# Prelude of a transformer block: the first modulation in blocks of 128 channels

## The chip, the cores and the metric

The kernel runs on one core of a Trainium2 chip, in one launch. The metric is device time in microseconds. Engines are named as in the profile: PE is TensorE (matmul), PEld its weight loads, DVE is VectorE, ACT is ScalarE, POOL is GpSimd, and SP is the queue that issues most transfers.

## The reference

One transformer block over 1024 tokens of width 1024, batch 1, fp32. What the prelude computes:

```python
mod = silu(c) @ w_mod + b_mod                       # c: [1, 1024], w_mod: [1024, 6 * 1024]
shift1, scale1, gate1, shift2, scale2, gate2 = split(mod, 6)
xn = x * rsqrt(mean(x * x, -1) + 1e-6) * ln1_g
u = xn * (1 + scale1) + shift1                      # [1024 tokens, 1024 channels]
proj = u @ w_in                                     # 5384 columns
```

`proj` feeds an attention branch, a linear-recurrence branch and gates; after them come an output projection, a second normalisation and a feed-forward part. Two column groups of `w_in` of 128 columns each, 24 and 25 in the kernel's numbering, are the low-rank projections of the recurrence; they are needed first.

## The kernel before

Channels lie on the 128 partitions and tokens along the free dimension, so u is held as `u_hi` and `u_lo` of shape [128, 8, 1024]: eight blocks of 128 channels (`kt`), two halves of 512 tokens (`half`). Each fp32 matrix is split into a rounded part (hi) and a remainder (lo), and a product is three products: hi hi, hi lo, lo hi.

The prelude is the `with` block that opens the pools `st` and `stp` (L403 to L545). In it the orders of SP, DVE and ACT are those of the program text, and PE's is so in the whole kernel. Instructions that follow in the text but lie outside the block may still be placed between them on SP, DVE, ACT and POOL, where the program's scheduler sees room.

- `load_x` (L408) loads eight tiles of 128 tokens, 512 KB each. `square` (L415) sums squares on ACT, `norm_x` (L421) makes 1/rms on ACT (`rms_rstd`, L285) and diagonal matrices `dg` on DVE (L426).
- `turn` (L456) multiplies x by `dg` on PE, which transposes and normalises: four fp32 products fill one PSUM bank for one block and one half. ACT copies it to `uf` (L511).
- `mod_load` (L428) loads eight tiles of w_mod for one part of the modulation, each 128 rows by 1024 columns. `mod_add` (L440) accumulates them on DVE: `acc = w[kt] * sc[kt] + acc` over 1024 columns, with `sc` = silu(c). `mod_sum` (L446) adds the partitions with eight one-column products on PE (`mps`) and adds the bias; for the scale it also forms `A1` = (1 + scale) * ln1_g. The scale (i = 1) is summed first, then the shift (i = 0).
- `u_steps` (L462): DVE applies A1 and the shift in place (L468), ACT rounds to `u_hi` (L469), DVE takes the remainder `u_lo` (L472).
- `low_part` (L475) multiplies u with both low-rank weights into four PSUM banks (`low`). Their own split is L527 (ACT) and L534 (DVE).
- `low_out` (L488) mixes neighbouring tokens of the result into `xwa` and `xg`.
- `warm(n)` (L435) issues n products into a bank that nobody reads.

The text of the prelude runs stage by stage: all squares and turns; the scale over all channels; the shift over all channels; then u and the low-rank products for half 0 and half 1. SP's order is x, the scale's tiles, the shift's tiles, the two low-rank weights, `w2`, `g2` and further constants.

After it comes the first large product, `ps_rkv`, by `shifted` (L346) with weights from `load_w` (L245): a load into one of two `raw` buffers (L249), a cast on ACT (L261), a remainder on DVE (L263). Those `raw` buffers are shared with the low-rank weights and `w2`. POOL makes `w2l` (L540) from `w2` and its cast (L537).

Of the kernel before, what the change touches and what calls it, by code (L numbers as in the profile page):

```python
# [44 lines left out]
NC1 = 384  # L45
# [86 lines left out]
def hybrid_block(ctx: ExitStack, tc: tile.TileContext, a, out):  # L132
    nc = tc.nc
# [3 lines left out]
    def mm(o, lhsT, rhs, start, stop, more=False):  # L137

        weave.mm_cost(o, lhsT, rhs)
        nc.tensor.matmul(o, lhsT, rhs, start=start, stop=stop, skip_group_check=more)  # L140
# [12 lines left out]
    rp = ctx.enter_context(tc.tile_pool(name="rp", bufs=2))  # L153
# [3 lines left out]
    wp = ww_st.enter_context(tc.tile_pool(name="wp", bufs=2, side="right"))  # L157
# [3 lines left out]
    cst = cp.tile([128, NC1], F32R, name="cst")  # L161
# [3 lines left out]
    def V(name, i=0, n=1):  # L165
        o, _ = VEC[name]
        return vec[:, o + i : o + i + n]
# [6 lines left out]
    ident, ones = f32(eye_r), f32(C("ones"))  # L174
# [16 lines left out]
    sc = cp.tile([128, 8], F32, name="sc")  # L191
# [112 lines left out]
    A1 = cp.tile([128, 8], F32, name="A1")  # L304
    m1 = cp.tile([128, 16], F32, name="m1")
# [3 lines left out]
    u_hi = upool.tile([128, KT, S], F32R, name="u_hi")  # L309
    u_lo = upool.tile([128, KT, S], F32R, name="u_lo")  # L310
# [24 lines left out]
    with ExitStack() as es:  # L335
# [67 lines left out]
        with tc.tile_pool(name="st", bufs=1) as st, tc.tile_pool(name="stp", bufs=2, space=PS) as stp, \  # L403
# [11 lines left out]
            def square(half, xs, js):  # L415
                for j in js:
                    t = half * 4 + j
                    nc.scalar.activation(uf[1][:, 6:8, :].rearrange("p k s -> p (k s)"), xs[j], AF.Square,
                                         accum_out=ssq[:, t : t + 1])

            def norm_x(half):  # L421

                hs = slice(half * 4, half * 4 + 4)
                rms_rstd(rstd[:, hs], ssq[:, hs])
                for j in range(half * 4, half * 4 + 4):
                    ts(dg[:, j, :], ident, rstd[:, j : j + 1], None, op0=ALU.mult)  # L426

            def mod_load(i, tags):  # L428
                ws = [st.tile([128, D], F32, tag=tags[kt % len(tags)], name=f"wm{i}{kt}", bufs={"mw": 4, "xt": 8}[tags[kt % len(tags)]])
                      for kt in range(KT)]  # L430
                for kt, w in enumerate(ws):
                    nc.sync.dma_start(w, a["w_mod"][kt * 128 : kt * 128 + 128, i * D : i * D + D])
                return ws, st.tile([128, D], F32, name=f"acc{i}")

            def warm(n):  # L435

                for _ in range(n):
                    mm(idle[:, 0:NC1], cst[:, 0:128], cst, start=True, stop=True)

            def mod_add(kt, ws, acc):  # L440
                if kt == 0:
                    ts(acc, ws[kt], sc[:, 0:1], None, op0=ALU.mult)
                else:
                    stt(acc, ws[kt], sc[:, kt : kt + 1], acc, op0=ALU.mult, op1=ALU.add)

            def mod_sum(i, acc):  # L446
                for j0 in (0, 4):
                    ps = stp.tile([128, 4], F32, tag="mp", name=f"mps{i}{j0}")
                    for j in range(4):
                        c0 = (j0 + j) * 128  # L450
                        mm(ps[:, j : j + 1], acc[:, c0 : c0 + 128], ones[:, 0:1], start=True, stop=True)
                    tt(m1[:, i * 8 + j0 : i * 8 + j0 + 4], ps, V("b_mod", i * 8 + j0, 4), op=ALU.add)
                    if i == 1:
                        stt(A1[:, j0 : j0 + 4], m1[:, 8 + j0 : 12 + j0], 1.0, V("ln1_g", j0, 4), op0=ALU.add, op1=ALU.mult)

            def turn(kt, half, xs):  # L456
                ps = stp.tile([128, NH], F32, tag="tp", name=f"tr{half}_{kt}")
                for j in range(4):
                    mm(ps[:, j * 128 : j * 128 + 128], xs[j][:, kt * 128 : kt * 128 + 128], dg[:, half * 4 + j, :], start=True, stop=True)
                return ps  # L460

            def u_steps(half):  # L462

                cs = slice(half * NH, half * NH + NH)
                for kt in range(KT + 1):
                    if kt < KT:
                        x = uf[half][:, kt, :]
                        ts(x, x, A1[:, kt : kt + 1], m1[:, kt : kt + 1], op0=ALU.mult, op1=ALU.add)  # L468
                        nc.scalar.copy(u_hi[:, kt, cs], x)  # L469
                    if kt > 0:  # L470
                        k = kt - 1
                        tt(u_lo[:, k, cs], uf[half][:, k, :], f32(u_hi[:, k, cs]), op=ALU.subtract)  # L472
                        yield k

            def low_part(kt, half, parts):  # L475
                for (wh, wl), ps in zip(low, low_ps):
                    for i in parts:
                        w, x = ((wh, u_hi), (wh, u_lo), (wl, u_hi))[i]
                        mm(ps[half], w[:, kt * 128 : kt * 128 + 128], x[:, kt, half * NH : half * NH + NH],
                           start=kt == 0 and i == 0, stop=kt == KT - 1 and i == 2)  # L480
# [21 lines left out]
            xs = [load_x(half) for half in range(2)]  # L502
            m = [mod_load(1, ("mw",)), None]
            uf = [st.tile([128, KT, NH], F32, name=f"uf{half}") for half in range(2)]
            warm(28)
            for half in range(2):
                square(half, xs[half], range(4))
                norm_x(half)
            for half in range(2):
                for kt in range(KT):  # L510
                    nc.scalar.copy(uf[half][:, kt, :], turn(kt, half, xs[half]))  # L511
            m[1] = mod_load(0, ("xt", "mw"))
            low_raw = [low_w(24, wp, ("whi", "wlo"), 2), low_w(25, st, ("xt", "xt"), 8)]
            low = [x[1:] for x in low_raw]
            w2 = rp.tile([128, S], F32, tag="raw", name="w2")
            for r in range(2):
                for j in range(2):
                    nc.sync.dma_start(w2[r * 64 : r * 64 + 64, j * 512 : j * 512 + 512], a["w2a2"][j * 64 : j * 64 + 64, :])
            nc.sync.dma_start(g2, a["g2"])
            nc.sync.dma_start(cst2, a["cst"][:, NC1:])  # L520
            for i in (1, 0):
                for kt in range(KT):
                    mod_add(kt, *m[1 - i])
                mod_sum(i, m[1 - i][1])
                warm((6, 40)[i])
            for raw, hi, _ in low_raw:
                nc.scalar.copy(hi, raw)  # L527
            low_ps = [[stp.tile([128, NH], F32, tag=("low", "tp")[hf], name=f"low{j}{hf}") for hf in range(2)] for j in range(2)]
            for half in range(2):
                for kt in u_steps(half):  # L530
                    low_part(kt, half, (0, 1))
                    if half == 0 and kt in (3, 5):
                        raw, hi, lo = low_raw[kt == 5]
                        tt(lo, raw, f32(hi), op=ALU.subtract)  # L534
                for kt in range(KT):
                    low_part(kt, half, (2,))
            nc.scalar.copy(w2h, w2)  # L537
# [1417 lines left out]
```

## Time and profile before

| What | us |
|---|---|
| Median of 3 runs (1702.5 to 1705.13) | 1702.53 |
| The profiled run's own time | 1703.54 |
| Its span, first to last instruction | 1701.4 |
| Transfers in the first 40 us | 13.81 MB |

A row of a timeline or of the chain begins with its start in us from the span's start and its duration; a group's row gives count, total busy time and the mean duration of one in ns. An instruction's duration is longer than the distance to the next independent one, since they overlap. In a row of windows the numbers are the stretch, its length, the busy time of PE, PEld, DVE, ACT and POOL with counts, the clock granted to TensorE, the share of the 16 transfer engines that was busy, and GB/s. A chain is what ended last, followed back; idle time of an engine counts only if it lies on it.

### The profile page before, as it was taken

The numbers are of one execution on the slowest core, as the hardware profiler recorded it, in microseconds if no ns is written. First come the engines' busy times: TensorE is split into PE (matmuls) and PEld (weight loads), VectorE is DVE, ScalarE is ACT, GpSimd is POOL, SyncE is SP. The second block draws the span as 40 slices with busy tenths as digits, with TensorE's granted clock in tenths as the row PEclk, the third lists the DMA queues.
The fourth block names the chain that finished last, engine by engine and source line by source line (L and its number), as shares of the span: only waits on it lengthen the run. The fifth ranks groups of instructions, "written<-read, shape, count | busy, mean of one in ns | idle before, by whom it ended". The sixth has DMA issues, their size and how long they took to land.

```text
span 1701.4 us, 26280 instructions
## 1 busy us (share of the span) xinstructions
PE 1649.4 (97%) x9886; PEld 1351.3 (79%) x9886; DVE 1216.2 (71%) x2390; ACT 810.2 (48%) x1482; POOL 145.7 (9%) x175
## 2 busy tenths in 40 slices
PE   7999999998999999999999999999999999999998
PEld 6767777686877777988878888888888888888886
DVE  5776786778676633888877634897777777787677
ACT  5553334434444555766642323654444444454455
POOL 0010101110111003123112000000000000000000
PEclk9999999999999999999999999999999999999999
DMA  8487743533332226443277611133332233484453
GB/s 328 146 307 210 189 121 97 134 109 107 91 115 76 83 89 151 139 120 100 75 272 269 238 62 63 50 106 98 120 111 100 93 118 101 152 296 150 128 211 114
DMA packets 120975, 239.87 MB, mean 141 GB/s; under 512 B 39888, under 2 KB 48336, under 8 KB 120848
## 3 DMA queue, kind: packets, MB, share of 16 engines
q1 hardware_dynamic: 112896, 220.94, 39.4%
q0 software_dynamic: 7952, 17.25, 3.7%
q8 instruction: 78, 1.28, 0.3%
q14 instruction: 49, 0.40, 0.1%
HBM read 172.59 MB, written 65.54 MB: 140 GB/s over the span
## 4 chain that ended last, share of the span: by engine, by line
PE 78%; DVE 10%; DMA 5%; ACT 3%; SPq 2%; issue 1%; DVEq 0%; ACTq 0%
PE X L140 13%; PE D L140 12%; PE Y L140 6%; PE wo L140 5%; PE br L140 5%; PE gt L140 5%; PE ps_rkv L140 4%; PE rk_ps L140 4%; PE W L140 3%; PE lg L140 2%; PE v L140 2%; PE ov L140 2%; PE qk L140 2%; PE sp L140 2%; PE tp L144 2%; PE tr L140 2%
## 5 line engine op out<-in xcount | busy, mean ns | idle before, releaser
L140 PE MATMUL D<-op,op 128*128 128x512 f32 x924 | 209.8, 389 | 0.0
L140 PEld LDWEIGHTS D<-op,op 128*128 128x128 f32 x924 | 173.3, 188 | 36.3 <-DVE op L1218 0.3
L140 PE MATMUL X<-T_m,S 128*128 128x512 f32 x440 | 107.2, 390 | 0.1
L140 PEld LDWEIGHTS X<-T_m,S 128*128 128x128 f32 x440 | 82.4, 188 | 18.2 <-ACT T_m L1643 0.6
L1217 ACT CAST op<-g 128x512 fp32r<-128x512 f32 x77 | 47.8, 621 | 73.4 <-PE D L140 48.2
L1218 DVE TENSOR_TENSOR op<-g,op 128x512 fp32r<-128x512 f32 x77 | 53.0, 688 | 41.3 <-ACT op L1217 41.3
L769 DVE TENSOR_TENSOR t<-E,M 128x60 f32<-128x60 f32 (+24 forms) x248 | 57.3, 231 | 33.1 <-DMA M<-sm 27.8
L1454 DVE SCALAR_TENSOR_TENSOR c<-ab,vec,c 128x512 f32<-128x512 f32 x88 | 65.9, 749 | 19.5 <-ACT c L1457 18.0
L263 DVE TENSOR_TENSOR lo_in<-raw_in,hi_in 128x512 fp32r<-128x512 f32 x84 | 56.4, 706 | 32.0 <-PE gt L140 13.8
L1418 DVE TENSOR_TENSOR S<-ur,S 128x512 fp32r<-128x512 f32 x66 | 45.5, 691 | 35.6 <-ACT S L1414 35.4
L1414 ACT CAST S<-ur 128x512 fp32r<-128x512 f32 x66 | 41.0, 622 | 55.5 <-DVE ur L1407 30.6
L261 ACT CAST hi_in<-raw_in 128x1024 fp32r<-128x1024 f32 x42 | 43.9, 1049 | 47.9 <-PE ps_rkv L140 16.8
L1418 DVE TENSOR_TENSOR A<-ur,A 128x512 fp32r<-128x512 f32 x64 | 44.0, 688 | 30.9 <-ACT A L1414 30.7
L140 PE MATMUL Y<-T_h,A 128*128 128x512 f32 x264 | 63.5, 389 | 0.0
L140 PE MATMUL Y<-T_h,S 128*128 128x512 f32 x264 | 63.3, 389 | 0.0
L140 PE MATMUL X<-B_b,A 128*128 128x512 f32 x252 | 60.8, 390 | 0.0
L140 PE MATMUL W<-B_f,A 128*128 128x512 f32 x252 | 60.6, 389 | 0.0
L771 DVE TENSOR_TENSOR E<-E,t 128x60 f32<-128x60 f32 (+24 forms) x248 | 53.8, 217 | 5.8
L1039 ACT ACTIVATE P<-lg,nm 128x896 f32<-128x896 f32 (+3 forms) x64 | 47.5, 744 | 21.9 <-DVE nm L1035 21.7
L140 PEld LDWEIGHTS Y<-T_h,A 128*128 128x128 f32 x264 | 49.6, 188 | 10.4
L140 PEld LDWEIGHTS Y<-T_h,S 128*128 128x128 f32 x264 | 49.6, 188 | 10.3
L1414 ACT CAST A<-ur 128x512 fp32r<-128x512 f32 x64 | 39.9, 623 | 34.3 <-PE X L140 31.5
(469 smaller groups left out, 4179.6 us busy)
## 6 DMA issues: line engine op xcount, KB each, us to landing
raw_in<-in_w_in SPq DMA_DIRECT2D x50, 512.0 KB, 4.1
wm<-in_w_mod SPq DMA_DIRECT2D x48, 512.0 KB, 6.6
ur<-in_w_up SPq DMA_DIRECT2D x44, 512.0 KB, 4.2
g<-d_g SPq DMA_DIRECT2D x35, 512.0 KB, 3.7
d_g<-gs SPq DMA_DIRECT2D x44, 256.0 KB, 2.0
d_g<-c SPq DMA_DIRECT2D x33, 256.0 KB, 4.6
d_st<-qh SPq DMA_DIRECT2D x64, 128.0 KB, 2.5
d_gate<-gs SPq DMA_DIRECT2D x32, 256.0 KB, 2.8
```

Of the source, the lines that this page charges most:

```text
L140: nc.tensor.matmul(o, lhsT, rhs, start=start, stop=stop, skip_group_check=more)
L144: nc.tensor.transpose(o, i, eye)
L261: nc.scalar.copy(hi, raw)
L263: nc.vector.tensor_tensor(lo[:, c : c + NH], raw[:, c : c + NH], f32(hi[:, c : c + NH]), op=ALU.subtract)
L769: tt(tv, E32[:, 0:J, s : s + 1].to_broadcast([128, J, W]), M32[:, s : s + 1, s + 1 : 32].to_broadcast([128, J, W]), op=ALU.mult)
L771: tt(E32[:, 0:J, s + 1 : 32], E32[:, 0:J, s + 1 : 32], tv, op=ALU.add)
L1039: nc.scalar.activation(e[:, 0:n], lg[:, 0:n], AF.Exp, bias=nm[:, 0:1], accum_out=nm[:, 1:2])
L1217: nc.scalar.copy(hi, src)
L1218: tt(lo, src, f32(hi), op=ALU.subtract)
L1414: nc.scalar.copy(hi, src)
L1418: tt(lo, src, f32(hi), op=ALU.subtract)
L1454: stt(c, ab[:, x + hf * NH : x + hf * NH + NH], V("conv_w", 22 * x + i), c, op0=ALU.mult, op1=ALU.add)
```

## The change

The modulation is cut by output channels. For block `kt`, `mod_load(kt)` loads two tiles of 512 KB, shift and scale, each holding all 1024 inputs for 128 output channels; a row of such a tile in memory is a run of 512 B. The scale is now summed by eight products per block on PE that accumulate in one PSUM column (`mod_scale`). The shift stays on DVE, in eight steps of 128 columns (`mod_shift`), with one product to add the partitions (`mod_sum`). `mod_col` forms the block's column of the shift and of A1. `u_upper` applies both on ACT, straight from the turn's PSUM bank, and rounds; `u_lower` takes the remainder on DVE. The low-rank products follow block by block, with all three parts at once. The low-rank weights' loads and splits come ahead of the second half of x, the splits around the first turn; w_mod has nine buffers, and the loads of blocks 4 to 7 are issued in the loop. `w2`, `g2` and the constants are loaded in block 4, and `w2` is cast in block 6. `warm` is called with 34, 10 and 16 in place of 28, 6 and 40.

```diff
-            def mod_add(kt, ws, acc):
-                if kt == 0:
-                    ts(acc, ws[kt], sc[:, 0:1], None, op0=ALU.mult)
-                else:
-                    stt(acc, ws[kt], sc[:, kt : kt + 1], acc, op0=ALU.mult, op1=ALU.add)
...
+            def mod_load(kt):
+
+                ws = [st.tile([128, D], F32, tag="mw", name=f"wm{i}{kt}", bufs=9) for i in range(2)]
+                for i, w in enumerate(ws):
+                    nc.sync.dma_start(w.rearrange("p (c n) -> p c n", n=128),
+                                      a["w_mod"].rearrange("(c p) n -> p c n", p=128)[:, :, i * D + kt * 128 : i * D + kt * 128 + 128])
+                return ws
...
+            def mod_scale(kt, ps):
+                for ci in range(KT):
+                    mm(ps[:, 1:2], mw[kt][1][:, ci * 128 : ci * 128 + 128], sc[:, ci : ci + 1], start=ci == 0, stop=ci == KT - 1)
+
+            def mod_shift(kt):
+                acc = st.tile([128, 128], F32, tag="acc", name=f"acc{kt}", bufs=2)
+                for ci in range(KT):
+                    w = mw[kt][0][:, ci * 128 : ci * 128 + 128]
+                    if ci == 0:
+                        ts(acc, w, sc[:, 0:1], None, op0=ALU.mult)
+                    else:
+                        stt(acc, w, sc[:, ci : ci + 1], acc, op0=ALU.mult, op1=ALU.add)
+                return acc
+
+            def mod_sum(kt, ps, acc):
+                mm(ps[:, 0:1], acc, ones[:, 0:1], start=True, stop=True)
+
+            def mod_col(kt, ps):
+                tt(m1.rearrange("p (i k) -> p k i", i=2)[:, kt, :], ps[:, 0:2],
+                   V("b_mod", 0, 16).rearrange("p (i k) -> p k i", i=2)[:, kt, :], op=ALU.add)
+                stt(A1[:, kt : kt + 1], m1[:, 8 + kt : 9 + kt], 1.0, V("ln1_g", kt), op0=ALU.add, op1=ALU.mult)
...
+            def u_upper(kt, half, ps):
+
+                uf[kt, half] = st.tile([128, NH], F32, tag="uf", name=f"uf{half}_{kt}", bufs=3)
+                nc.scalar.activation(uf[kt, half], ps, AF.Identity, scale=A1[:, kt : kt + 1], bias=m1[:, kt : kt + 1])
+                nc.scalar.copy(u_hi[:, kt, half * NH : half * NH + NH], uf[kt, half])
+
+            def u_lower(kt, half):
                 cs = slice(half * NH, half * NH + NH)
...
+                tt(u_lo[:, kt, cs], uf[kt, half], f32(u_hi[:, kt, cs]), op=ALU.subtract)
+
+            def low_part(kt, half):
+                for i in (0, 2, 1):
+                    for (wh, wl), ps in zip(low, low_ps):
                         w, x = ((wh, u_hi), (wh, u_lo), (wl, u_hi))[i]
...
+            def low_split(n, engine):
+                raw, hi, lo = low_raw[n]
+                if engine == "ACT":
+                    nc.scalar.copy(hi, raw)
+                else:
+                    tt(lo, raw, f32(hi), op=ALU.subtract)
+
+            def mods(kt):
+                ps = pb.tile([128, NH], F32, tag="big", name=f"mod{kt}")
+                mod_scale(kt, ps)
+                acc = mod_shift(kt)
+                mod_sum(kt, ps, acc)
+                mod_col(kt, ps)
...
+            uf = {}
+            xs = load_x(0)
+            mw = [mod_load(0)]
+            low_raw = [low_w(24, wp, ("whi", "wlo"), 2), low_w(25, st, ("hi25", "lo25"), 1)]
...
+            xs += load_x(1)
+            mw += [mod_load(kt) for kt in range(1, 4)]
+            warm(34)
+            for t in range(4):
+                square(t)
+            norm_x(0)
+            low_ps = [[stp.tile([128, NH], F32, tag="low", name=f"low{j}{hf}", bufs=4) for hf in range(2)] for j in range(2)]
+            mods(0)
+            low_split(0, "ACT")
+            u_upper(0, 0, turn(0, 0))
+            warm(10)
+            low_split(0, "DVE")
+            low_split(1, "ACT")
+            low_split(1, "DVE")
+            blocks = [(kt, half) for kt in range(KT) for half in range(2)]
+            for n, (kt, half) in enumerate(blocks):
+                if n == 0:
+
+                    u_lower(kt, half)
+                    low_part(kt, half)
+                    for t in range(4, 8):
+                        square(t)
+                    norm_x(1)
+                    warm(16)
+                if n < len(blocks) - 1:
+                    u_upper(*blocks[n + 1], turn(*blocks[n + 1]))
+                if n:
+                    u_lower(kt, half)
+                    low_part(kt, half)
+                if half == 0 and kt < KT - 1:
+                    mods(kt + 1)
+                    if kt < 4:
+                        mw.append(mod_load(kt + 4))
+                if kt == 4 and half == 0:
...
+                if n == 12:
+                    nc.scalar.copy(w2h, w2)
```

More of the change, by code (lines that the diff above doesn't have):

```diff
@@ L413, in load_x, with square @@
                 return xs
[L415 to L419, printed above, removed]
+            def square(t):
+                nc.scalar.activation(u_lo[:, 6 + t // 4, :], xs[t], AF.Square, accum_out=ssq[:, t : t + 1])
             def norm_x(half):
@@ L438, in warm @@
                     mm(idle[:, 0:NC1], cst[:, 0:128], cst, start=True, stop=True)
-            def mod_add(kt, ws, acc):
-                if kt == 0:
-                    ts(acc, ws[kt], sc[:, 0:1], None, op0=ALU.mult)
-                else:
[L444 to L454, printed above, removed]
@@ L457, in turn @@
+            def mod_sum(kt, ps, acc):
[4 more added lines that the diff above has]
+                stt(A1[:, kt : kt + 1], m1[:, 8 + kt : 9 + kt], 1.0, V("ln1_g", kt), op0=ALU.add, op1=ALU.mult)
+            def turn(kt, half):
                 ps = stp.tile([128, NH], F32, tag="tp", name=f"tr{half}_{kt}")
@@ L458, in turn @@
                 for j in range(4):
-                    mm(ps[:, j * 128 : j * 128 + 128], xs[j][:, kt * 128 : kt * 128 + 128], dg[:, half * 4 + j, :], start=True, stop=True)
+                    mm(ps[:, j * 128 : j * 128 + 128], xs[half * 4 + j][:, kt * 128 : kt * 128 + 128], dg[:, half * 4 + j, :], start=True, stop=True)
                 return ps
-            def u_steps(half):
-                cs = slice(half * NH, half * NH + NH)
[L465 to L473, printed above, removed]
@@ L500, in hybrid_block @@
             dg = xwa.rearrange("p (j s) -> p j s", s=128)
             idle = pb.tile([128, NH], F32, tag="big", name="idle")
[L502 to L511, printed above, removed]
@@ L521, in hybrid_block @@
[L521 to L536, printed above, removed]
@@ new lines, in hybrid_block @@
+            mods(0)
[24 more added lines that the diff above has]
+                if kt == 4 and half == 0:
+                    w2 = rp.tile([128, S], F32, tag="raw", name="w2")
+                    for r in range(2):
+                        for j in range(2):
+                            nc.sync.dma_start(w2[r * 64 : r * 64 + 64, j * 512 : j * 512 + 512], a["w2a2"][j * 64 : j * 64 + 64, :])
+                    nc.sync.dma_start(g2, a["g2"])
+                    nc.sync.dma_start(cst2, a["cst"][:, NC1:])
+                if n == 12:
+                    nc.scalar.copy(w2h, w2)
```

21 lines of the change are left out of this document (1 added, 20 removed).

## The prediction

> **What bounds the kernel now.** I read the page first, then the chain of waits over the first 120 us, then the timeline of that stretch by engine, then groups and windows for prices.
>
> ```profile
> span 1701.4 us, 26280 instructions
> PE 1649.4 (97%) x9886; PEld 1351.3 (79%) x9886; DVE 1216.2 (71%) x2390; ACT 810.2 (48%) x1482; POOL 145.7 (9%) x175
> ```
>
> TensorE is busy for 97% of the span, so a microsecond taken from the prelude only counts if the moment from which TensorE runs without gaps comes earlier. That moment is the first product of `ps_rkv`; its row, and the last low-rank row before it, from the timeline:
>
> ```profile
> 71.33 3.84 PE L140 MATMUL low<-u_hi,lo_in 128*128 128x512 f32 x16
> ...
> 75.01 1.99 PE L140 MATMUL ps_rkv<-u_hi,hi_in 128*128 128x512 f32 x8
> ```
>
> So the prelude ends at 75.0 us. What made it that long, from the chain:
>
> ```profile
> 9.97 0.07 ACT uf L418
> ...
> 12.76 1.16 ACT uf L418 x2
> 13.94 1.16 ACT uf L418 x2
> ...
> 16.30 0.31 ACT rstd L287
> ...
> 16.84 0.48 ACT uf L511
> ...
> 17.36 13.05 PE tr L140 x112
> ...
> 33.41 1.30 DVE acc L444
> ...
> 41.34 1.30 DVE acc L444
> ...
> 62.32 1.06 ACT hi_in L261
> ```
>
> The stages stand one behind the other: TensorE turns x until 30.4, VectorE sums the shift from 32.6 to 42.6 with TensorE on filler, then VectorE makes u and the low-rank products trail it. The last row is a cast of the next stage's weights on ScalarE: it lies in that queue between two casts of u, and ScalarE had stood waiting for its transfer.
>
> **The change: TensorE.** A product of two fp32 operands shows as two records: `mod_sum` issues 8 products, and its row has 16.
>
> ```profile
> 30.37 1.95 PE L140 MATMUL mps<-cst,acc 128*128 128x1 f32 x16
> ```
>
> One such product costs 1.95 / 8 = 0.244 us though it has a single column. A `turn` (4 products, 8 of the 112 records in 13.05 us) costs 0.93. A low-rank product costs (75.01 - 71.33) / 16 = 0.230. The change adds 64 products for the scale (15.6 us) and keeps 8 sums in place of 16 (-1.95); turns and low-rank products stay in number. It also drops filler: 60 instead of 74 matmuls. For one block of channels TensorE now has 2 turns (1.86), 12 low-rank products (2.76), 8 scale products (1.95) and one sum (0.24): **6.82 us**, and its order is fixed, so the next block cannot overtake.
>
> **The change: VectorE and ScalarE.** VectorE loses the scale's eight passes and the 16 in-place affine steps (L468), and gets the shift in 64 small steps.
>
> ```profile
> L444 DVE SCALAR_TENSOR_TENSOR acc<-wm,sc,acc 128x1024 f32<-128x1024 f32 x14 | 18.0, 1285 | 3.2 <-DMA wm<-in_w_mod 2.7
> L1454 DVE SCALAR_TENSOR_TENSOR c<-ab,vec,c 128x512 f32<-128x512 f32 x88 | 65.9, 749 | 19.5 <-ACT c L1457 18.0
> L771 DVE TENSOR_TENSOR E<-E,t 128x76 f32<-128x76 f32 x8 | 1.9, 236 | 0.2
> 11.72 0.87 DVE L426 TENSOR_SCALAR xwa<-cst,rstd 128x128 f32<-128x128 f32 x4 [8.45 <-ACT rstd L288]
> L426 DVE TENSOR_SCALAR xwa<-cst,rstd 128x128 f32<-128x128 f32 x8 | 1.7, 282 | 12.7 <-ACT rstd L288 12.7
> L472 DVE TENSOR_TENSOR u_lo<-uf,u_hi 128x512 fp32r<-128x512 f32 x16 | 11.0, 686 | 0.6 <-ACT u_hi L469 0.5
> L469 ACT CAST u_hi<-uf 128x512 fp32r<-128x512 f32 x16 | 9.6, 619 | 12.1 <-DVE uf L468 12.1
> L1329 ACT ACTIVATE uf_e<-tr,m,A 128x512 f32<-128x512 f32 x8 | 6.2, 787 | 8.3 <-PE tr L140 8.3
> L527 ACT CAST hi_in<-raw_in 128x1024 fp32r<-128x1024 f32 x2 | 2.1, 1044 | 10.3 <-DMA raw_in<-in_w_in 10.3
> ```
>
> No row has a 128x128 step of this form. The line through 1024 and 512 elements gives 0.35 us at 128; the 76-element row bounds it below at 0.24. In a dependent chain 0.04 is added (six steps of L444 from 33.41 to 41.34 are 1.32 apart, each 1.285). Eight steps, the first 0.28 + 0.04: 2.2 to 3.0 us; I take 3.0, the line of the same operation. The affine step moves to ScalarE, straight from PSUM, at 0.79 (L1329 is the same operation) in place of a 0.59 copy. Per block VectorE has 3.0 + 2 x 0.6 + 0.4, ScalarE 2 x (0.79 + 0.62): both lie beside TensorE's 6.82. The wait to check is the round trip. From the start of a turn: 0.93, affine 0.79, cast 0.62, u_lo 0.69, shift 3.0, handoffs 0.2 make 6.2, and TensorE reaches that sum at 6.58. It holds with 0.35 us to spare; shift steps over 0.40 us would end that.
>
> **The change: transfers.** The bytes are the same, but each w_mod tile now comes as 1024 pieces of 512 B in place of 128 of 4 KB. The nearest row is the d_v store, whose pieces are 512 B; beside it two stretches of w_mod reads in 4 KB rows:
>
> ```profile
> DMA packets 1056, 0.52 MB, mean 87 GB/s; under 512 B 32, under 2 KB 1056, under 8 KB 1056
> 357.50:358.00 0.50, 0.50 (x14) 0.43 (x16) 0.50 (x2) 0.00 (x0) 0.00 (x0) 1.00 0.97 293
> 18.00:29.00 11.00, 11.00 (x98) 11.00 (x97) 8.12 (x7) 6.83 (x12) 0.00 (x0) 1.00 0.90 294
> 29.00:40.00 11.00, 10.36 (x69) 9.90 (x67) 9.03 (x11) 1.38 (x3) 0.00 (x0) 1.00 1.01 404
> ```
>
> With the engines full, 512 B pieces moved at 293 GB/s and 4 KB rows at 404. I take 293 for reads too; the bounds are 404, and half of 293 for a read that no row shows. A pair of tiles (1.05 MB) then takes 3.6 us (a tile 1.8), under 6.82, so transfers bind only at the start. The Trainium skill ("DMA: Bandwidth & Descriptors", Specifications) puts the least size for full rate at 512 B; by that a pair would take 2.6 us, the sum below would stay (VectorE's first shift, not the transfer, ends last there), and the second rival would lose its chance to the forecast. The row, a store, speaks for less than full rate.
>
> On SP the two low-rank weights pass four x tiles, which come 1.05 MB / 404 = 2.6 us later; the square steps they feed wait for ScalarE until 19.5 anyway. The loads of blocks 4 to 7 wait on SP for buffers that shift and scale of earlier blocks free; behind them stand w2, g2, the second constants and the first weights of `ps_rkv`, all needed only from about 63 us (the cast of w2 in block 6). POOL keeps its two w2l steps.
>
> **The sum.** The fourth x tile is there at 9.97 (its square starts). Block 0's tiles follow at 13.55. VectorE ends dg at 12.6 and shift 0 at 15.6; TensorE ends scale 0 at 15.5, its sum at 15.95 and the first turn at 16.9. ScalarE then has affine 0.79, cast 0.62, the second weight's cast 1.04, four squares 1.18 apart and 0.54 for the rstd: 24.7. dg lets the second turn run from 25.0 to 25.95, scale 1 until 27.9, but shift 1 (25.6 to 28.6) ends last; its sum ends at 28.95. Six blocks of 6.82 follow: 69.85. Behind the sum of block 7 stand turn, low-rank, turn, low-rank (4.62: 74.5); the last half's u_lo is ready at 73.1 + 0.79 + 0.62 + 0.69 + 0.15 = 75.35, and two products more make 75.8. That is 0.8 later than 75.01. The weights cast that sat in ScalarE's and VectorE's queues (1.06, then 1.29) will sit somewhere in the new loop too, against 0.35 to spare: +0.9. The low-rank outputs now all come at the end: 0 to 0.75, taken as 0.3. Together **+2.0 us**: a span of 1703.4, 1705.5 for the profiled run (1703.54 with its span of 1701.4), 1704.5 against the median of 1702.53.
>
> What 15.6 us of scale products add on TensorE thus eats nearly all that the overlap of the stages wins.
>
> **Rivals.** First, *a cast of weights stalls the loop* (slower). The raw buffer of the first `ps_rkv` weights is free once the low-rank weights are split, about 20.6, so the load can be issued there, behind the last x tile (13.55 + 2.6 + 5.2 = 21.4) and nine w_mod tiles: 21.4 + 9 x 1.8 + 1.3 for itself = 39 until it lands. If its cast sits early in ScalarE's queue, everything behind it stands. Before, this wait was:
>
> ```profile
> ACT hi_in L261 <- DMA raw_in<-in_w_in: 3.5, 1, 3.5
> 42.77 2.99 PE L140 MATMUL mps<-cst,acc 128*128 128x1 f32 x16 [3.41 <-DVE acc L444]
> 44.00:45.00 1.00, 1.00 (x7) 1.00 (x6) 0.16 (x1) 0.00 (x0) 0.00 (x0) 0.50 0.00 0
> 49.00:50.00 1.00, 1.00 (x4) 0.81 (x3) 1.00 (x3) 0.62 (x1) 0.00 (x0) 0.50 0.00 0
> ```
>
> A wait as long again costs 3.5 less 0.8: 1707. A cast placed at 27.5 waits 11 us, and after the gap of 3.41 us the granted clock was 0.50 until 50, some 7 us, 3.5 us more: 1718. Middle: 1711. It decides from a wait of some 2.5 us. For it: it happened before; against: with more in its queue the load may be placed later.
>
> Second, *512 B reads at half the store's rate*, 146 GB/s: a pair takes 7.2 us, all w_mod (8.39 MB) takes 57.5 us, and behind the first x tiles (9.97) and beside 3.15 MB at 404 (7.8) block 7 lands at 75.3; with 1.95, 0.24 and the 6.0 from there to the end the prelude ends at 83.5: 1711. For it: no row shows such a read. Against it: the slower stretch of 4 KB reads still made 294 on engines 0.90 full.
>
> Third, *the summing products are cheap* (faster): were one product in an accumulating group 0.12 (its neighbour's load hidden) and a shift step 0.27, a block would take 5.7, the prelude end near 68.5: 1697. Against it: in the row of `mps` 8 products left 16 records 0.122 apart, and each has its own weights.
>
> **Numbers.** Forecast 0.48, stalled cast 0.27, slow reads 0.14, cheap products 0.11. About 0.2% (3.4 us) is what a measurement tells from no change: 1699.1 to 1705.9. The forecast's own spread (-3 to +3) leaves 0.42 within and 0.06 above; the two slower rivals give 0.39 above and 0.02 within; the third 0.11 below. Range 1699 to 1713; the forecast's own is 1701.5 to 1707.5.
>
> **What would show it.** Right: 128 records of 128x1 for the scale (two per product), 0.12 apart; starts of the last sums of two blocks 6.8 us apart; TensorE without gaps from about 29; first `ps_rkv` product at 75 to 77. The cast: an idle time of ScalarE before L261 that ends with raw_in. Reads: TensorE's scale products waiting for wm. Wrong altogether: a period clearly under 6.8 us, or a first `ps_rkv` product before 72.

## The result and the profile after

| | before | after |
|---|---|---|
| median (runs; lowest to highest) | 1702.25 us (6; 1700.97 to 1705.13) | 1715.26 us (6; 1713.60 to 1719.88) |
| ratio, 95% interval | | 1.0067 [1.0054, 1.008] |
| profiled run, its span | 1703.54, 1701.4 | 1715.42, 1713.2 |
| mean granted clock of that run | 0.990 | 0.986 |
| first `ps_rkv` product | 75.01 | 88.04 |

One of the nine runs of a_pin_wide below took 4140.17 us; medians and ratios leave it out.

The change made the kernel 13 us slower, 10.8 us above the forecast and 2.3 above the range. All of it is there when the prelude ends. These rows of TensorE's timeline of the changed kernel (start, duration, engine, operation; idle time before it and what ended it) are the summing products of blocks 1, 2, 4, 5, 6 and 7, the first product after the longest idle time, and the first product of the next stage:

```profile
29.06 0.38 PE L140 MATMUL mod<-cst,acc 128*128 128x1 f32 x2 [0.65 <-DVE acc L450]
...
37.26 0.36 PE L140 MATMUL mod<-cst,acc 128*128 128x1 f32 x2
...
50.45 0.36 PE L140 MATMUL mod<-cst,acc 128*128 128x1 f32 x2
...
58.24 1.22 PE L140 MATMUL low<-u_hi,hi_in 128*128 128x512 f32 x2 [4.14 <-ACT u_hi L471]
...
64.23 0.56 PE L140 MATMUL mod<-cst,acc 128*128 128x1 f32 x2
...
73.72 0.36 PE L140 MATMUL mod<-cst,acc 128*128 128x1 f32 x2
...
81.34 0.38 PE L140 MATMUL mod<-cst,acc 128*128 128x1 f32 x2 [0.88 <-DVE acc L450]
...
88.04 1.99 PE L140 MATMUL ps_rkv<-u_hi,hi_in 128*128 128x512 f32 x8
```

The sum of block 1 came at 29.06, where the forecast had 28.95. From block 2 to block 4 two periods took 50.45 - 37.26 = 13.19, 6.60 each (forecast 6.82). Then one block took 13.78 and the next 9.49. The idle time of 4.14 us ends with a cast of `u` on ScalarE. ScalarE's timeline shows what held that cast up, and the chain of waits what it waited for:

```profile
48.35 0.62 ACT L471 CAST u_hi<-uf 128x512 fp32r<-128x512 f32 x1
55.81 1.04 ACT L261 CAST hi_in<-raw_in 128x1024 fp32r<-128x1024 f32 x1 [6.84 <-DMA raw_in<-in_w_in]
56.76 0.77 ACT L470 ACTIVATE uf<-tr,m,A 128x512 f32<-128x512 f32 x1
```

```profile
49.23 6.56 DMA raw_in<-in_w_in
```

The cast of the next stage's first weights stands in ScalarE's queue behind the rounding of `u` of block 3, second half, which ended at 48.97. Its load was issued only at 49.23, so ScalarE stood for 6.84 us, and behind the cast stood the affine step of block 4. SP's queue says why the load came so late: it lies behind the last w_mod tile, four pieces of w2, g2 and the second constants (start, duration on the queue).

```profile
44.48 3.54 SPq L560 DMA_DIRECT2D w<-in_w2a  x4
48.06 0.58 SPq L561 DMA_DIRECT2D g<-in_g  x1
48.69 0.43 SPq L562 DMA_DIRECT2D cst<-in_cst  x1
```

The gap cost more than itself. In the windows of the changed kernel (stretch; its length; busy time and instructions of PE, PEld, DVE, ACT, POOL; granted clock; DMA share; GB/s) the clock is at half from 57 to about 70:

```profile
57.00:60.00 3.00, 1.76 (x4) 1.49 (x5) 2.86 (x7) 2.45 (x4) 0.00 (x0) 0.50 0.23 55
60.00:63.00 3.00, 3.00 (x14) 2.72 (x13) 1.68 (x5) 0.00 (x0) 0.00 (x0) 0.50 0.32 120
63.00:66.00 3.00, 3.00 (x15) 3.00 (x16) 0.92 (x3) 0.00 (x0) 0.00 (x0) 0.50 0.00 0
66.00:69.00 3.00, 3.00 (x10) 2.50 (x9) 0.79 (x2) 1.40 (x2) 0.00 (x0) 0.50 0.01 3
69.00:72.00 3.00, 3.00 (x15) 2.67 (x14) 2.56 (x8) 1.15 (x2) 0.00 (x0) 0.76 0.02 5
```

There are two shorter drops earlier, at 16 to 19 and at 29 to 33, with no idle time of more than 0.65 us beside them:

```profile
16.00:18.00 2.00, 2.00 (x10) 2.00 (x10) 1.32 (x3) 0.35 (x1) 0.00 (x0) 0.50 1.03 410
18.00:20.00 2.00, 2.00 (x10) 2.00 (x9) 0.00 (x0) 1.97 (x4) 0.00 (x0) 0.69 1.01 394
...
30.00:32.00 2.00, 2.00 (x9) 1.81 (x9) 0.44 (x1) 0.74 (x1) 0.00 (x0) 0.50 1.19 294
```

So there were two suspects: the cast that waits (rival 1 of the prediction), and a clock that falls for some other reason. The experiments separate them.

### The profile page after: what moved, and what is told of

It reads as the page before. It is cut to its first block, busy times and chain, and to the rows that moved or that the text cites. A ratio compares the mean times of both kernels' runs of the same rounds, so it can differ in the third digit from the quotient of the medians.

```text
span 1713.2 us, 26506 instructions
## 1 busy us (share of the span) xinstructions
PE 1665.3 (97%) x9984; PEld 1367.0 (80%) x9984; DVE 1213.0 (71%) x2432; ACT 813.1 (47%) x1482; POOL 143.5 (8%) x175
## 4 chain that ended last, share of the span: by engine, by line
PE 80%; DVE 9%; DMA 4%; ACT 3%; SPq 2%; issue 1%; DVEq 0%; ACTq 0%; POOLq 0%
PE X L140 13%; PE D L140 12%; PE Y L140 6%; PE wo L140 5%; PE gt L140 5%; PE br L140 5%; PE ps_rkv L140 5%; PE qk L140 4%; PE rk_ps L140 4%; PE W L140 3%; PE lg L140 2%; PE ov L140 2%; PE tr L140 2%; PE sp L140 2%; PE tp L144 2%
## 5 line engine op out<-in xcount | busy, mean ns | idle before, releaser
L261 ACT CAST hi_in<-raw_in 128x1024 fp32r<-128x1024 f32 x42 | 43.9, 1047 | 52.5 <-PE ps_rkv L140 17.2
```

## The experiments

The kernels were run in three groups (the first four rows, the next four, the last three); each ratio is to runs of the kernel before on the same chip, whose medians were 1704.17 (22 runs), 1704.42 (31) and 1705.61 (23). The last column is the mean over the runs of each run's granted clock (the changed kernel 0.9870; before 0.9886, 0.9886 and 0.9883); the first `ps_rkv` product is that of the profiled run.

| kernel | median | ratio, 95% interval | first `ps_rkv` | granted clock |
|---|---|---|---|---|
| a_pin | 1711.92 | 1.0039 [1.0023, 1.0055] | 75.78 | 0.9889 |
| a_pin_wide | 1709.05 | 1.0027 [1.0014, 1.004] | 77.03 | 0.9901 |
| a_fill | 1713.80 | 1.0062 [1.0045, 1.0079] | 85.32 | 0.9885 |
| b_pin | 1708.10 | 1.0017 [1.0006, 1.0027] | 72.51 | 0.9878 |
| a_mid2_r | 1709.60 | 1.0029 [1.0017, 1.004] | 78.95 | 0.9885 |
| a_wait_r | 1709.16 | 1.0021 [1.0009, 1.0033] | 78.38 | 0.9893 |
| a_pin_one_r | 1709.86 | 1.004 [1.0025, 1.0054] | 76.88 | 0.9882 |
| b_mid_r | 1704.73 | 0.9998 [0.9988, 1.0008] | 71.73 | 0.9884 |
| a_mix | 1707.53 | 1.0007 [0.9994, 1.002] | 75.47 | 0.9897 |
| a_thin | 1712.86 | 1.0047 [1.0035, 1.006] | 79.95 | 0.9853 |
| b_best | 1702.40 | 0.9988 [0.9976, 0.9999] | 73.01 | 0.9909 |

**a_pin: the cast held behind the last rounding of u.** Only the order in ScalarE's queue changes.

```diff
-            nc.scalar.copy(hi, raw)
+            i = nc.scalar.copy(hi, raw)
+            if "u" in marks:
+                tc.add_manual_dep(i.ins, marks["u"].ins.name, NOSYNC)
...
-                nc.scalar.copy(u_hi[...], uf[kt, half])
+                marks["u"] = nc.scalar.copy(u_hi[...], uf[kt, half])
```

> The changed kernel with one order kept: the casts of the next stage's weights on ScalarE (L261) stay behind the last rounding of u. Theory (the stalled cast and the half clock behind it cost 4.1 + 5.8 of the 13 us): no gap of TensorE near 54, no clock of 0.50 after 57, the first ps_rkv product at 77 to 79 in place of 88.0, time 1703.5 to 1706.5. Rival (the 64 scale products on TensorE and the block order cost it): the first ps_rkv product stays above 84, time 1710 or more.

TensorE's timeline of a_pin:

```profile
28.49 0.38 PE L140 MATMUL mod<-cst,acc 128*128 128x1 f32 x2 [0.65 <-DVE acc L452]
35.11 0.36 PE L140 MATMUL mod<-cst,acc 128*128 128x1 f32 x2
...
48.29 0.36 PE L140 MATMUL mod<-cst,acc 128*128 128x1 f32 x2
54.89 0.36 PE L140 MATMUL mod<-cst,acc 128*128 128x1 f32 x2
61.48 0.36 PE L140 MATMUL mod<-cst,acc 128*128 128x1 f32 x2
69.09 0.38 PE L140 MATMUL mod<-cst,acc 128*128 128x1 f32 x2 [0.88 <-DVE acc L452]
75.78 1.98 PE L140 MATMUL ps_rkv<-u_hi,hi_in 128*128 128x512 f32 x8
```

The wait, the gap and every drop of the clock before 95 us are gone, and the stage ends at 75.78. Set beside the changed kernel's rows, this divides the 12.26 us between the two: +0.57 at the sum of block 1 and +1.58 more at block 2 (the two early drops, 2.15; 2.39 counted from the sum of block 0, which came 0.24 earlier in the changed kernel), nothing to block 4, then +7.18 at block 5 and +2.90 at block 6 (10.08, of which 4.14 is the idle time and 5.94 half clock), and nothing after that. But the median came down by far less: a_pin's eight runs lie between 1706.95 and 1715.86, and its profile is one of the fastest, 1707.41. Its interval touches that of the changed kernel (1.0054 to 1.0055); those of a_wait_r and a_mid2_r below, whose casts are moved by less, are clear of it. So a second cause was left.

**a_fill: filler in the gap instead.** 24 filler products before the low-rank products of block 4, first half; the cast stays where it was.

```diff
+                if n == 8:
+                    warm(24)
```

> The changed kernel with the cast left where it stalls, and 24 filler products (about 4.25 us) on TensorE just ahead of the low-rank products that wait for it (block 4, half 0). If the half clock is a cost of its own, the granted clock stays 1.00 from 54 to 72, and of the 13 us some 5.8 go: 1708.5 to 1711, with the wait of ScalarE (6.8 us) unchanged. If only the wait counts: 1714 to 1716.

Mostly a miss: the median falls by some 1.5 us at most, inside the intervals. The cast now waited 8.19 us, TensorE still idled 1.32 us after 4.41 us of filler, and two short drops of the clock remained (61 to 65, 78 to 82). Filler shortened the half clock, but the wait stays.

**b_pin: the kernel before with its cast held back in the same way.**

```diff
-                        nc.scalar.copy(u_hi[:, kt, cs], x)
+                        marks["u"] = nc.scalar.copy(u_hi[:, kt, cs], x)
```

> The kernel before with the same order kept: its casts L261 stay behind its last rounding of u. If its own wait of 3.5 us before L261 lay on the path, the first ps_rkv product comes at 71 to 72 in place of 75.0 and the time is 1698.0 to 1699.5. If VectorE sets the pace there and the cast's and the split's work only moves to the end, it changes by less than 1.5 us.

A miss: `ps_rkv` starts 2.5 us earlier (72.51), but `zp`, a product behind `ps_rkv`, only at 90.84 (before 89.76). The raw buffer is now freed late, the next cast waits 4.70 us for its load, and VectorE's work stands behind it. TensorE idles from 83.6 to 86.2 until VectorE has read a `ps_rkv` bank, and the clock drops behind it. ScalarE's row of that cast, and TensorE's of the product that waits:

```profile
72.13 1.05 ACT L261 CAST hi_in<-raw_in 128x1024 fp32r<-128x1024 f32 x1 [4.70 <-DMA raw_in<-in_w_in]
```

```profile
86.17 3.21 PE L140 MATMUL ps_rkv<-u_hi,hi_in 128*128 128x512 f32 x8 [2.58 <-DVE k L360]
```

The wait had only moved to the next load. (In a_pin this has a trace as well: a gap of 0.64 us at 87.46.)

**a_mid2_r and a_wait_r: where does a wait begin to cost?** The cast behind block 5, first half, where its load has landed; and behind block 4, first half, where it has not. In both its split on VectorE is kept behind `u_lo` of block 5, second half.

```diff
+                if (kt, half) == (5, 0):      # a_wait_r: (4, 0)
+                    marks["u"] = i
```

> The changed kernel with the first cast of weights kept behind the rounding of u of block 5, first half, and its split on VectorE behind u_lo of the second half, so that the raw buffer is free early but nothing waits for the load. In the kernel with the cast held to the end (a_pin) raw_in was issued at 47.18 and that rounding ended at 57.7; with 6.56 us from issue to use the load is there at 53.8. Theory (a cast ahead of its load was the whole loss): no idle time of ScalarE before L261 beyond 0.3 us, first ps_rkv product at 75.8 to 76.8 (the 1.04 us of the cast against 0.35 spare), a load of the next weights issued some 5 us before 76.59, no gap before r's products, zp at 90.0 to 91.0; median 1705 to 1710, as a_pin or up to 1 us less. Rival (whatever sits in the loop costs, because every engine's queue is tight): first ps_rkv product at 78 or later, and TensorE below full clock after it.

> The same with the cast two roundings earlier, behind u_hi of block 4, first half, which ended at 51.13 in a_pin: the wait for raw_in should be 2.7 us instead of 6.84. Theory by threshold (the prediction put the point from which a wait decides at 2.5 us): the next affine step comes 2.9 us late, the low-rank products that need it have some 1.1 us to spare, so TensorE has one gap of 1.5 to 2 us and no half clock behind it; first ps_rkv product at 77.3 to 78.0, median some 2 us over the one with the cast behind block 5. Rival (any gap over about 1 us drops the clock for several us): half clock from a few us after the gap, first ps_rkv product at 80 to 84, median 5 to 8 us over the one with the cast behind block 5.

In a_mid2_r the cast ran at 57.91 without a wait and the periods stayed 6.59 (sums at 28.77, 35.39, 41.98, 48.58, 55.17, 61.76): a cast of 1.04 us in this loop costs nothing. In a_wait_r, from the timelines of ScalarE and TensorE:

```profile
54.57 1.05 ACT L261 CAST hi_in<-raw_in 128x1024 fp32r<-128x1024 f32 x1 [3.37 <-DMA raw_in<-in_w_in]
```

```profile
57.00 0.73 PE L140 MATMUL low<-u_hi,hi_in 128*128 128x512 f32 x2 [0.67 <-ACT u_hi L475]
```

A wait of 3.37 us (2.7 was expected) left a gap of 0.67; the wait of 6.84 left 4.14. Both differences are 3.47, so in these two traces TensorE stands for what exceeds 2.70 us. The block took 0.93 us longer in all (62.48 - 54.96 = 7.52 for 6.59), less than the expected gap of 1.5 to 2. No drop of the clock followed the 0.67. The medians are equal, where some 2 us between them were expected; a difference of 0.93 is less than they can tell. Both first `ps_rkv` products came later than expected (78.95 for 75.8 to 76.8, 78.38 for 77.3 to 78.0), since both kernels' profiles have half clock at another place, one piece in a_wait_r and two in a_mid2_r, from 69 to 75:

```profile
68.00:70.00 2.00, 1.12 (x8) 1.04 (x8) 1.32 (x2) 0.00 (x0) 1.93 (x2) 0.70 0.00 0
70.00:72.00 2.00, 2.00 (x9) 2.00 (x10) 1.09 (x3) 0.09 (x1) 0.50 (x1) 0.50 0.36 45
72.00:74.00 2.00, 2.00 (x6) 1.52 (x6) 0.63 (x1) 1.30 (x2) 0.00 (x0) 0.50 0.92 328
74.00:76.00 2.00, 2.00 (x11) 1.89 (x10) 0.06 (x1) 0.01 (x1) 0.00 (x0) 0.59 0.98 365
```

There the eight scale products of block 7, an idle time of 0.88 and the summing product make one stretch of about 3 us in which TensorE does little. a_pin has the same stretch (its 0.88 stands above) and no drop, so it does not happen every time.

**a_pin_wide and a_pin_one_r: the scale products.** a_pin with 64 equal columns in each scale product; and a_pin with one of the eight, which leaves seven eighths of the scale's sum out.

```diff
-                    mm(ps[:, 1:2], mw[...], sc[:, ci : ci + 1], ...)
+                    mm(ps[:, 1:65], mw[...], sc[:, ci : ci + 1].to_broadcast([128, 64]), ...)
```

```diff
-                for ci in range(KT):
+                for ci in range(1):
...
```

> As a_pin, and each scale product has 64 equal columns (sc repeated) in place of one, into unused columns of the same bank. Theory (one-column products count as little activity, so that the clock drops behind them at 16 to 19 and 29 to 33 us): the granted clock is 1.00 there, and the time is 1.5 to 3 us below a_pin. Rival (those drops come from the gaps beside them): same clock rows, time from 0 to 1 us above a_pin.

> a_pin with one of the eight scale products of each block (the other seven 128-channel parts of the sum for the scale are left out). Forecast's bound (TensorE with its fixed order, 0.244 us for each fp32 product, VectorE's round trip close behind): 1.7 us less TensorE work for a block, but the round trip of 6.2 then ends last, so the period falls from 6.59 to 6.0 to 6.3; first ps_rkv product at 72.0 to 73.8 (a_pin 75.78). If TensorE alone set it the period would be 4.9 and the first ps_rkv product at 64 to 66. If VectorE's round trip alone set it already: 6.5 to 6.6, no change. Of the clock: if the one-column products are what lets it drop in some runs of a_pin (1707 to 1716), the runs here lie within 4 us of each other; if not, they spread by 7 us or more as there.

The wide form decided nothing: its interval overlaps that of a_pin, and neither profile has a drop in the prelude. In a_pin_one_r the third case of the expectation came, not the forecast's bound. Two of its summing products:

```profile
42.94 0.38 PE L140 MATMUL mod<-cst,acc 128*128 128x1 f32 x2 [1.34 <-DVE acc L452]
49.47 0.38 PE L140 MATMUL mod<-cst,acc 128*128 128x1 f32 x2 [1.34 <-DVE acc L452]
```

With seven products less for TensorE in each block (1.5 us by the 1.70 that eight take between two starts, 35.56 to 37.26 in the changed kernel) the period is 6.53, and TensorE waits 1.34 us for VectorE's shift. The round trip through ScalarE and VectorE is thus 6.53 long, not 6.2, and nearly as long as TensorE's own 6.59. The spread did not shrink either (1706.66 to 1715.62). In its profile the clock dropped from 28 to 35, beside an idle time of 2.22 us before the sum of block 1 (26.16 to 28.38): fewer thin products, but longer waits.

**a_thin and a_mix: thin stretches on TensorE.** Both are a_mid2_r with one thing changed. a_thin has 1 filler product instead of 10 and of 16 in the early stage. a_mix puts the low-rank products between the scale products and the sum.

```diff
-            warm(10)
+            warm(1)
...
-                    warm(16)
+                    warm(1)
```

```diff
+                if half == 0 and kt < KT - 1:
+                    ps = pb.tile([128, NH], F32, tag="big", name=f"mod{kt + 1}")
+                    mod_scale(kt + 1, ps)
                 if n:
                     u_lower(kt, half)
                     low_part(kt, half)
                 if half == 0 and kt < KT - 1:
-                    mods(kt + 1)
+                    acc = mod_shift(kt + 1)
+                    if n == 0:
+                        warm(3)
+                    mod_sum(kt + 1, ps, acc)
+                    mod_col(kt + 1, ps)
```

> a_mid2_r with 1 filler product in place of 10 and 1 in place of 16 between 16.8 and 25 us. No path waits for these products, so the first turn, the sum of block 1 and the period should stay; only the clock can change. Theory (thin stretches of TensorE trip it): half clock in at least two pieces of 3.4 us between 18 and 35 in the profiled run, first ps_rkv product 1.5 to 4 us later than it would be without them, median 1711 to 1714 beside 1709.6 of a_mid2_r. Rival (only idle times of 3.4 us and more count): TensorE would be idle for some 2.5 us at a time here, no half clock, median as a_mid2_r.

> The changed kernel with its first cast of weights behind block 5 and its split behind u_lo (as in a_mid2_r), and in each block the six low-rank products of the first half put between the eight scale products and the summing product on TensorE, so that one-column products, the wait for VectorE and the summing product no longer stand in one stretch of 2.3 to 3.0 us; three filler products before the sum of block 1. The work and the order on the other engines stay. In the profiles so far half clock came in pieces of about 3.4 us, each costing 1.7 us: two pieces early in the changed kernel, two at 68 to 76 in a_mid2_r, one at 71 in a_wait_r, none in a_pin and a_pin_wide. Theory (a stretch of thin TensorE work trips the clock when it happens to fill most of one such piece): no half clock between 10 and 90, first ps_rkv product at 75.8 to 76.5, and the median falls from 1709.6 to 1704.5 to 1706.5 beside 1704.4 before. Rival (the pieces of half clock do not depend on the order of the products, but on TensorE's whole load): half clock at the same places, median 1708.5 to 1710.5.

Windows of a_thin, and the longest idle time of its TensorE there:

```profile
18.00:20.00 2.00, 0.50 (x1) 0.19 (x1) 0.35 (x1) 1.97 (x3) 0.00 (x0) 1.00 1.01 397
20.00:22.00 2.00, 1.20 (x3) 0.58 (x3) 1.75 (x2) 1.97 (x4) 0.00 (x0) 0.78 1.19 310
22.00:24.00 2.00, 1.68 (x4) 0.83 (x3) 0.08 (x1) 1.94 (x5) 0.00 (x0) 0.50 1.22 289
...
32.00:34.00 2.00, 2.00 (x9) 1.84 (x9) 0.46 (x1) 0.58 (x1) 0.00 (x0) 0.50 1.21 293
```

```profile
25.76 2.08 PE L140 MATMUL tr<-xwa,xt 128*128 128x128 f32 x8 [2.08 <-DVE xwa L428]
```

Half clock from about 21 to 35. Ahead of it TensorE had worked 1.7 of 4 us, with no idle time longer than 1.34 us; the one of 2.08 came later, within the drop. Its median is the highest of the kernels without a waiting cast, and the expected 1711 to 1714 came. The six runs had a granted clock of 0.984 to 0.986, the twelve of a_mid2_r 0.986 to 0.991, so the drop was not the profiled run's alone. Windows of a_mix over the whole prelude:

```profile
10.00:30.00 20.00, 18.78 (x121) 16.83 (x120) 11.29 (x32) 11.56 (x21) 0.00 (x0) 1.00 1.14 337
30.00:50.00 20.00, 20.00 (x141) 18.27 (x140) 12.83 (x36) 8.63 (x13) 0.00 (x0) 1.00 1.15 274
50.00:70.00 20.00, 19.18 (x137) 17.34 (x135) 14.97 (x38) 9.61 (x14) 2.54 (x2) 1.00 0.19 68
```

Full clock throughout, `ps_rkv` at 75.47, `zp` at 89.43 (before 89.76), and a ratio whose interval includes 1. The median is a little above the expected 1704.5 to 1706.5, but before stood 1.2 us higher in this group; the ratio is the better reading. a_thin and a_mix are clearly apart; a_mid2_r is only nearly apart from either (its interval shares 1.0017 to 1.002 with a_mix and 1.0035 to 1.004 with a_thin).

**b_mid_r and b_best: a faster kernel before.** The cast behind block 5 of the second half; and with it 56 filler products instead of 40 ahead of the last sums.

```diff
+                        if (kt, half) == (5, 1):
+                            marks["u"] = i
```

```diff
-                warm((6, 40)[i])
+                warm((6, 56)[i])
```

> The kernel before with its first cast of weights behind the rounding of u of block 5 of the second half instead of behind block 1, where it waited 3.49 us for its load. Theory: the load lands at about 62, the rounding ends at 62.8, so the wait is under 0.5 us; first ps_rkv product at 72.5 to 73.2 (before 75.01; 72.51 with the cast held to the end), the raw buffer is free early enough, so the products of r have no gap, zp at 87.3 to 88.2 (before 89.76); median 1701.5 to 1703 where before has 1704.2, 1 to 2.5 us less. Rival (the loads of the next weights set the end whatever the first cast does, as with the cast held to the end): zp at 89.5 or later, median as before.

> The kernel before with the cast behind block 5 of the second half (as in b_mid_r) and 56 filler products in place of 40 ahead of the last sums of the modulation, where TensorE stood idle for 3.4 us (39.4 to 42.8) and had half clock from 43 to 50 in every profile of the kernel before. 16 more at 0.18 us fill 2.9 us of it. Theory: no half clock at 43 to 51 (two pieces, 3.4 us, in before; one, 1.7, in b_mid_r), first ps_rkv product at 69.8 to 71.0 (before 75.01, b_mid_r 71.73), median 1700.5 to 1702.5 beside 1704.4 before: the fastest version. Rival (time won in the prelude is given back later by the clock, as the median of b_mid_r, equal to before's in spite of 3.3 us won in its profile, may say): first ps_rkv as above but median 1703.5 to 1705.

In b_mid_r the first cast no longer waits (the next one waits 2.70 us); `ps_rkv` starts at 71.73 and `zp` at 86.47, 3.3 us earlier. Of this 1.3 us is there ahead of the cast's old place (one low-rank product at 55.18 for 56.48), where its profile has one piece of half clock for two. The cast's share is the other 2.0 us, no more than the interval leaves open (0.9988). The median is that of before, not the expected 1701.5 to 1703. b_best closes the idle time of 3.41 us to 0.63, and is the only kernel whose interval lies below 1:

```profile
43.82 1.92 PE L140 MATMUL mps<-cst,acc 128*128 128x1 f32 x16 [0.63 <-DVE acc L446]
```

Its `ps_rkv` missed the expected time (73.01 for 69.8 to 71.0): in that run one piece of half clock at 17 to 21 lengthened the turns (14.68 us for 13.05), so that the first sums came 1.15 us later, and another came at 48 to 51 although the idle time ahead of it was closed. Its median is within the expected range, but before stood 1.2 us higher in this group; by the ratio the gain is 2 us.

## Why the prediction was wrong

**The step that failed** is the sentence on SP's queue: behind the loads of blocks 4 to 7 stand "w2, g2, the second constants and the first weights of `ps_rkv`, all needed only from about 63 us". The first weights were needed at 48.97, because their cast had its place in ScalarE's queue there, ahead of block 4. The forecast priced that cast at its length (+0.9) and left its wait to rival 1 with a chance of 0.27. The rival had the load landing at 39; it was issued at 49.23, behind all of w_mod, w2, g2 and the second constants, and landed 6.56 later, at 55.8. The trace of before had shown such a wait (3.49 us before L261). A load and the cast that reads it lie in two queues that are ordered apart: with the change the cast's turn came 9.86 us earlier (48.97 for 58.83), and the load's issue only 6.64 earlier (49.23 for 55.87). The rival's own remark, that with more in its queue "the load may be placed later", was put down as a point against it; it was the point for it.

**Rival 1 was right in mechanism and short in size.** Its point of decision, 2.5 us, measured 2.70. It had a wait of 3.5 for 1707 and 11 us for 1718; 6.84 us gave 1715.26, of which 2.15 are the early drops. The term that was mis-sized is the half clock behind the gap: "some 7 us, 3.5 us more" was read off the gap of 3.41 in before; after 4.14 us it lasted 13 us and cost 5.94.

**What held.** The 512 B pieces moved at 289 to 294 GB/s where the engines were full (293 taken from the store): rival 2 did not come. The Trainium skill ("DMA: Bandwidth & Descriptors", Specifications) has 512 B as the least size for the full rate; beside the 404 of 4 KB rows this does not hold here. The shift steps, 2.99 us for eight, as taken. Rival 3 did not come: eight scale products took 1.70 us, and the period is 6.59, not 5.7.

**What held by luck.** The period of 6.82 was argued from TensorE with 0.35 us to spare; the spare was 0.06 (6.59 for TensorE, 6.53 for the round trip). TensorE's terms were off both ways: the scale products took 1.70 (1.95 in the sum) and the two turns 1.70 (1.86), but the twelve low-rank products 2.97 (2.76). "What 15.6 us of scale products add on TensorE thus eats nearly all" is therefore only half true: taking seven of eight away (a_pin_one_r) won 0.06 us for a block. The start agreed in the changed kernel (sum of block 1 at 29.06 for 28.95) only with an early drop of the clock in it; in a_pin it was 28.49. And with the cast out of the way the first `ps_rkv` product came at 75.78 (a_pin), where the sum gave 75.8, but the parts do not agree so well: the start was 0.46 us earlier, the six blocks took 0.3 less, and what follows the sum of block 7 took 6.69 for 5.95. The +0.9 for the cast was 0 (a_mid2_r), and the +0.3 for the low-rank outputs was 0: from `ps_rkv` to `zp` it is 14.75 before and 14.72 in a_pin.

**What was not in the prediction** is the half clock that comes without a long idle time. The forecast asked for a TensorE without gaps from 29 us and took that for full clock. In the changed kernel it cost 2.15 us in the profiled run. That a stretch in which TensorE does little brings it on is shown by a_thin, in its trace and in the clock of all its runs. That the order of the products matters is made likely by a_mix (0.9897 for 0.9885 in a_mid2_r). Which of the stretches trips in a given execution was not settled.

**What stays open** is why a_pin, a_mid2_r and a_wait_r are still 0.2 to 0.4% above before, where the forecast had 0.1%. For the half clock: in a_mid2_r's profile the two pieces at 69 to 75 make up most of the 3.94 us by which its `ps_rkv` comes after that of before, and within a_pin the time goes with the clock (1706.95 and 1707.41 at 0.992, 1715.86 at 0.986). Against it: the three kernels' granted clock (0.9889, 0.9885, 0.9893) is no lower than that of before (0.9886). And a_pin's profile has no half clock ahead of 95 us and the same seven pieces from there to the last product as before, yet its span is 3.6 us longer (1705.0 for 1701.4), of which only 0.77 is there at the first `ps_rkv` product.

## What to carry to other kernels

When a change moves work in one queue, list for each load the instruction that reads it and that instruction's place in its own engine's queue: a cast placed early in front of a load placed late stops everything behind it, and holding the cast back too far only moves the wait to the load that needs its buffer. A wait costs what exceeds the slack of the loop (2.70 us here), and, where the gap it leaves is long (4.14 us here, not 0.67), again through the clock. A stretch in which TensorE does little can bring half clock without a long idle time; a_thin shows it for few products, and for products of one column with short waits it is likely. Dense products between them are worth a try.

## What the hardware showed

Half clock comes in pieces of about 3.4 us. Counted over the whole trace in stretches of 1 us, every drop lost 1.7 us or a multiple of it (one or two pieces, four behind the gap of 4.14 and in a_thin). The Trainium skill ("TensorE: Matmul & The Clock Gate", Part 1) has the gate judge activity in windows of some 3.4 us; the length agrees. Its advice to avoid idle times of more than that is not enough here: drops stand beside an idle time of 2.22 us in a_pin_one_r, shorter ones with few products between them in a_thin, and 0.88 between thin products in a_mid2_r, which brought none in a_pin.

The same places of the program lose one piece in one execution and two or none in another: near 232 us one or two, near 300 none, one or two, near 499 one or none. Up to the last product the profiled runs have between seven pieces (a_pin, a_mix; 12 us of lost clock) and fourteen (a_pin_one_r; 24 us). The difference is of the order of the spread between runs of one kernel (8.9 us in a_pin), and may be the reason that what b_mid_r won in its prelude does not show in its median.

VectorE's shift steps start 0.39 us apart, but beside GpSimd's split of w2 the row of seven steps stretches; VectorE's row, its last step alone, and GpSimd's row:

```profile
77.51 3.77 DVE L450 SCALAR_TENSOR_TENSOR acc<-wm,sc,acc 128x128 f32<-128x128 f32 x7
```

```profile
79.84 1.45 DVE L450 SCALAR_TENSOR_TENSOR acc<-wm,sc,acc 128x128 f32<-128x128 f32 x1
```

```profile
79.88 2.59 POOL L567 TENSOR_TENSOR w2l<-w,w2h 64x512 fp32r<-64x512 f32 x2 [77.92 <-ACT w2h L564]
```

Elsewhere these seven steps take 2.68; the 1.09 us more are behind the idle time of 0.88 before the sum of block 7. All of it is in the last step: it starts at 79.84 and takes 1.45 us, where the six before it take 0.35 each, and GpSimd's first instruction runs beside it. It is the same in a_pin and a_mix. No run moves the split, so that GpSimd is the cause is likely, not shown.
